# Two of four v chunk pairs by Strassen's seven products, bias by an adding DMA, in a two-layer decoder trunk

## The chip, the core and the metric

The kernel runs on one core of a Trainium2 chip. The metric is the device time of one execution in microseconds (us), the median of several runs. The engines named below are PE (TensorE: matmuls and transposes), PEld (its weight loads), DVE (VectorE), ACT (ScalarE), POOL (GpSimd) and SP (SyncE, which issues DMAs here). Each engine works through its own instructions in a fixed order and waits where an input is not there yet.

## What is computed

The input is one sequence of 256 rows of width 2048. Layer one is attention: RMS norm, an input projection, two mixers with a bias on the scores, an output projection and the residual. Layer two, in which most of the change lies, is this, cut from the reference:

```python
h = _rms(x, ln_g)                               # 256 x 2048
z = h @ w_in                                    # w_in: 2048 x 12288
uv = jax.nn.gelu(z[..., :2 * C_WIDTH])          # C_WIDTH = 4096
gate = jax.nn.silu(z[..., 2 * C_WIDTH:])
u, v = uv[..., :C_WIDTH], uv[..., C_WIDTH:]
v = _rms(v, v_g)                                # needs all of a row of v
ws = w_s * np.tril(np.ones((128, 128)))
s = jnp.einsum('gts,bnsgc->bntgc', ws, v) + b_s
y = u * s * gate
return x + y @ w_out                            # w_out: 4096 x 2048
```

## The kernel before

All products are made from float32 values split in two parts, a rounded high part (hi, type fp32r) and the rest (lo). A product is then three matmuls: hi x hi, hi x lo of the weights, lo x hi of the weights (L121 to L123).

`gemm` works on one **chunk**, 512 columns of a weight matrix. The rows stand in two halves of 128 (two accumulators in PSUM, one for each half), and the 2048 of the inner dimension in 16 k tiles of 128. `wtile` loads two k tiles of weights at a time (512 KB, on SP's queue, L81, six buffers `wraw`), ACT rounds them into `whi` (L85) and DVE subtracts to get `wlo` (L86), four buffers each. One such tile feeds 2 k tiles x 2 halves x 3 = 12 matmuls of 128x512, so a chunk has 96.

The first layer: input projection chunks, with attention spread between their matmuls by `fill()`, which takes one step of a queue of generators. Each of eight `bias_tile` calls loads 512 KB of bias on POOL's queue (L271) and adds the mask with POOL (L272). Then comes the output projection of four chunks (lines from L541). After each, `resid` adds the accumulators to the residual `xr` (DVE L518) and takes squares (ACT L520); `next_hT` transposes the new `xr` (PE L529, four transposes into one PSUM bank, two banks in a chunk), and makes from it, in pieces of 128x256, `hTh` (ACT L535, scaled) and `hTl` (DVE L536), the left side of the next layer. The last of the four chunks thus has its `next_hT` after it, among the matmuls of the first v chunk. `row_rstd` makes the row scale from a chain of tiny DVE operations.

The second layer begins with the eight v chunks (the **v stage**, from 436 us on): a gemm, Gelu by ACT (L191), squares (L574), load of v_g on POOL's queue (L576), multiplication by it on POOL (L577). All v tiles stay in SBUF. After the eighth, the row scale of v is known, and for each of eight chunks come u and gate gemms with the spatial mixing `sgu` between their matmuls; then the last projection, `w_out1`.

The instructions are put on the engines in an order that a scheduler makes ahead of time from the program; the rows of that order are shown in the section on the change.

Of the kernel before, what the change touches and what calls it, by code (L numbers as in the profile page):

```python
# [33 lines left out]
def trunk(ctx, tc, x, xT, ev_g, w_in0, w_kva, qk_g, sinks, w_out0, od_g, w_in1, v_g, w_sT, b_s,  # L34
# [8 lines left out]
    ps = ctx.enter_context(tc.tile_pool(name="ps", bufs=4, space=bass.MemoryType.PSUM))  # L43
# [13 lines left out]
    def psum(tag, bufs):  # L57
        return ps.tile([P, 512], F32, tag=tag, bufs=bufs, name=nm(tag))
# [16 lines left out]
    def wtile(w, kt, cw, fine=False):  # L75
# [7 lines left out]
        for j in range(0, 2, step):  # L83
            js = slice(j, j + step)
            nc.scalar.copy(hi[:, js, :cw], raw[:, js, :cw])  # L85
            nc.vector.tensor_tensor(lo[:, js, :cw], raw[:, js, :cw], hi[:, js, :cw].bitcast(F32),  # L86
                                    op=ALU.subtract)
        return hi, lo
# [11 lines left out]
    def gemm(aT, nkt, w, cw, pre=None, last=False):  # L100
# [25 lines left out]
        return acc if last else [g[0] for g in acc]  # L126

# [393 lines left out]

    def next_hT(q):
        hi, lo = c4([P, 4, S], nm("hTh"), F32R), c4([P, 4, S], nm("hTl"), F32R)
        for p0 in range(0, 4, 2):
            tp = psum("s", 2)
# [5 lines left out]
            for j in range(2):  # L531
                kt = 4 * q + p0 + j
                gk = g1[:, kt:kt + 1]
                src = tp[:, j * 256:(j + 1) * 256]
                nc.scalar.activation(hi[:, p0 + j, :], src, AF.Copy, scale=gk)  # L535
                nc.vector.scalar_tensor_tensor(lo[:, p0 + j, :], src, gk,  # L536
                                               hi[:, p0 + j, :].bitcast(F32),
                                               op0=ALU.mult, op1=ALU.subtract)
            if p0:
                hT1[q] = (hi, lo)  # L540
            yield  # L541

# [11 lines left out]
    nc.scalar.dma_start(bst, b_s)  # L554

# [10 lines left out]
    in1 = lambda c: gemm(yTk(hT1), KT, w_in1[c], 512)  # L566
    ssv = cons.tile([P, 2, 8], F32, name="ssv")
    vt = []
    for c in range(8):
        acc = in1(8 + c)  # L570
        v = evac(acc, 512, AF.Gelu, rs=rs1, name="v")
        for tt in range(2):
            junk = m2([P, 512], nm("junk"))
            nc.scalar.activation(junk, v[:, tt, :], AF.Square, accum_out=ssv[:, tt, c:c + 1])  # L574
        gv = m2([P, 512], nm("gv"))
# [121 lines left out]
```

## Time and profile before

| | us |
|---|---|
| median of 3 runs (1158.7 to 1159.94) | 1159.05 |
| the profiled execution | 1158.9 |
| its span, first to last instruction | 1157.1 |
| PE busy in it | 1149.3 |
| DVE busy | 641.3 |
| ACT busy | 592.7 |
| POOL busy | 115.5 |

The difference between the execution and its span lies around the program, before its first and after its last instruction. In a row of the timeline the first number is the start in us from the start of the span, the second the busy time, then engine, line, operation, tile written from tiles read, its shape, and in square brackets how long the engine had been idle before it and what ended that. The ends of matmuls are modelled: one row is 0.39 us long where the next starts 0.23 us later, so the distance of starts is what a matmul costs. A row with x2 or x4 is several instructions in one.

### The profile page before, as it was taken

The page shows a single profiled execution, that of the slowest core. Times are in us where ns is not written, and L with a number is a line of the kernel's source. Part 1 is how long each engine was busy: PE and PEld are TensorE (multiplying, and loading weights), DVE is VectorE, ACT ScalarE, POOL GpSimd, SP SyncE. Part 2 cuts the span into 40 slices and gives each one's busy share as a digit, 9 for nine tenths or more (in the row PEclk, how much of TensorE's full clock was granted, in tenths as well). Part 3 has the DMA queues.
Part 4 walks back from the last instruction along what each step waited for, and adds up shares of the span by engine and source line. Part 5 has one row for each costly group of instructions (what it writes and reads, how often), then busy time and mean ns, then how long its engine had stood idle before and what let it go on. Part 6 is the DMA issues. An engine that isn't in the chain of part 4 may idle for free.

```text
span 1157.1 us, 14468 instructions
## 1 busy us (share of the span) xinstructions
PE 1149.3 (99%) x5498; PEld 952.8 (82%) x5498; DVE 641.3 (55%) x823; ACT 592.7 (51%) x820; POOL 115.5 (10%) x69
## 2 busy tenths in 40 slices
PE   9999999999999999999999999999999999999998
PEld 7887787788788888888888888888888888888887
DVE  6586567556546565544546555555555555445443
ACT  6556664644654455445445445554554455333432
POOL 0132112113012000111110000000000000000000
PEclk9999999999999999999999999999999999999999
DMA  9676435546447555666666555555556555666661
GB/s 352 224 248 208 130 117 184 172 137 226 144 143 228 185 183 182 215 204 200 213 203 193 184 181 187 177 184 194 185 168 197 182 184 172 203 207 210 197 210 38
DMA packets 63638, 218.37 MB, mean 189 GB/s; under 512 B 7632, under 2 KB 10320, under 8 KB 63312
## 3 DMA queue, kind: packets, MB, share of 16 engines
q1 hardware_dynamic: 60352, 209.74, 56.2%
q0 software_dynamic: 2080, 7.34, 2.1%
q8 instruction: 43, 0.70, 0.2%
q10 hardware_dynamic: 1136, 0.36, 0.1%
q14 instruction: 27, 0.22, 0.1%
HBM read 215.32 MB, written 2.10 MB: 188 GB/s over the span
## 4 chain that ended last, share of the span: by engine, by line
PE 95%; DVE 1%; ACT 1%; DMA 1%; issue 1%; SPq 0%; ACTq 0%
PE g L121 30%; PE g L122 30%; PE g L123 30%; PE t L331 1%; DMA wraw<-in_w_in_dram 1%; ACT whi L85 1%; DVE wlo L86 1%; PE s L298 1%; PE u L347 1%; PE u L346 1%; PE t L385 1%; PE u L345 0%; PE t L218 0%; PE s L599 0%; PE s L600 0%
## 5 line engine op out<-in xcount | busy, mean ns | idle before, releaser
L86 DVE TENSOR_TENSOR wlo<-wraw,whi 128x1024 fp32r<-128x1024 f32 (+1 forms) x393 | 512.7, 1309 | 448.8 <-ACT whi L85 447.7
L85 ACT CAST whi<-wraw 128x1024 fp32r<-128x1024 f32 (+1 forms) x393 | 408.3, 1041 | 490.8 <-PE g L123 468.0
L121 PE MATMUL g<-whi,hTh 128*128 128x512 f32 (+1 forms) x1184 | 464.2, 392 | 0.0
L122 PE MATMUL g<-wlo,hTh 128*128 128x512 f32 (+1 forms) x1184 | 459.5, 388 | 0.6 <-DVE wlo L86 0.6
L123 PE MATMUL g<-whi,hTl 128*128 128x512 f32 (+1 forms) x1184 | 458.9, 388 | 0.0
L123 PEld LDWEIGHTS g<-whi,hTl 128*128 128x128 f32 x1184 | 222.6, 188 | 45.0
L121 PEld LDWEIGHTS g<-whi,hTh 128*128 128x128 f32 x1184 | 222.8, 188 | 44.6
L122 PEld LDWEIGHTS g<-wlo,hTh 128*128 128x128 f32 x1184 | 222.8, 188 | 44.0 <-DVE wlo L86 1.4
L121 PE MATMUL g<-whi,yTh 128*128 128x512 f32 (+1 forms) x416 | 156.2, 376 | 0.0
L122 PE MATMUL g<-wlo,yTh 128*128 128x512 f32 (+1 forms) x416 | 155.3, 373 | 0.0
L123 PE MATMUL g<-whi,yTl 128*128 128x512 f32 (+1 forms) x416 | 155.3, 373 | 0.0
L123 PEld LDWEIGHTS g<-whi,yTl 128*128 128x128 f32 x416 | 78.3, 188 | 14.1
L121 PEld LDWEIGHTS g<-whi,yTh 128*128 128x128 f32 x416 | 78.4, 188 | 13.6
L122 PEld LDWEIGHTS g<-wlo,yTh 128*128 128x128 f32 x416 | 78.4, 189 | 13.5
L608 POOL TENSOR_TENSOR y<-y,gt 128x1024 f32<-128x1024 f32 x8 | 19.2, 2404 | 344.9 <-ACT gt L191 344.9
L577 POOL TENSOR_TENSOR v<-v,gv 128x1024 f32<-128x1024 f32 x8 | 22.1, 2757 | 219.5 <-ACT junk L574 219.5
L191 ACT ACT_TABLE_LOAD x20 | 25.7, 1283 | 1.7 <-PE g L123 1.4
L272 POOL TENSOR_TENSOR bias<-bias,ba 128x1024 f32<-128x1024 f32 x8 | 21.9, 2738 | 31.1 <-DMA bias<-in_bias_dram 27.8
L321 ACT ACTIVATE pr<-sb,nmx 128x256 f32<-128x256 f32 x32 | 16.2, 506 | 9.9 <-DVE nmx L319 6.6
L333 ACT COPY pt<-t 128x384 f32<-128x384 f32 x32 | 15.0, 469 | 9.8 <-PE t L331 9.8
L307 DVE CUSTOM_DVE_ANT_0 sb<-s,bias 128x256 f32<-128x256 f32 x32 | 13.3, 414 | 9.1 <-PE s L301 8.1
L588 DVE SCALAR_TENSOR_TENSOR vl<-v,rstdv,vh 128x512 fp32r<-128x512 f32 x16 | 11.3, 749 | 12.4 <-ACT vh L587 12.4
(127 smaller groups left out, 555.2 us busy)
## 6 DMA issues: line engine op xcount, KB each, us to landing
wraw<-in_w_in_dram SPq DMA_DIRECT2D x287, 512.0 KB, 3.7
wraw<-in_w_out_dram SPq DMA_DIRECT2D x96, 512.0 KB, 4.0
bias<-in_bias_dram POOLq DMA_DIRECT2D x8, 512.0 KB, 3.8
xT<-in_xT_dram SPq DMA_DIRECT2D x8, 256.0 KB, 5.0
xr<-in_x_dram SPq DMA_DIRECT2D x2, 1024.0 KB, 11.1
wraw<-in_w_kva_dram SPq DMA_DIRECT2D x8, 256.0 KB, 3.4
gv<-in_v_g_dram POOLq DMA_DIRECT2D x8, 256.0 KB, 3.1
out_dram<-o SPq DMA_DIRECT2D x7, 256.0 KB, 5.1
```

Of the source, the lines that this page charges most:

```text
L85: nc.scalar.copy(hi[:, js, :cw], raw[:, js, :cw])
L86: nc.vector.tensor_tensor(lo[:, js, :cw], raw[:, js, :cw], hi[:, js, :cw].bitcast(F32), op=ALU.subtract)
L121: nc.tensor.matmul(o, ah[:, sl], whi[:, k, a:b], start=st, stop=False)
L122: nc.tensor.matmul(o, ah[:, sl], wlo[:, k, a:b], start=False, stop=False)
L123: nc.tensor.matmul(o, al[:, sl], whi[:, k, a:b], start=False, stop=en)
L191: nc.scalar.activation(z[:, tt, :cw], acc[tt][:, :cw], func, scale=rs[:, tt:tt + 1])
L272: nc.gpsimd.tensor_tensor(bt, bt, ba[:, mix:mix + 1, :].broadcast_to([P, 4, 256]), op=ALU.add)
L307: nc.vector.tensor_tensor_reduce(out=sb[:, 0:256], in0=sp[:, 0:256], in1=bt[:, j, :], scale=1.0, scalar=NEG, op0=ALU.add, op1=ALU.max, acc ...
L321: nc.scalar.activation(pr[:, 0:256], sb[:, 0:256], AF.Exp, bias=nmx[:, j, 1:2], accum_out=l[:, j, 1:2])
L333: nc.scalar.copy(pt, tp[:, 0:384])
L577: nc.gpsimd.tensor_tensor(v, v, gv.unsqueeze(1).broadcast_to([P, 2, 512]), op=ALU.mult)
L608: nc.gpsimd.tensor_tensor(y, y, gate[0], op=ALU.mult)
```

## The change

The eight v chunks are chunks 8 to 15 of `w_in1`. Chunks 8 and 9 form a pair, and so do 12 and 13; chunks 10, 11, 14 and 15 stay plain. With rows halved (a1*, a2*), the inner dimension halved by even and odd k tiles, and the two chunks as column halves, a pair is a 2 x 2 block product, and `four_chunks` computes it by seven products instead of eight:

- p1 = a11 b11, p2 = a12 b21, p3 = (sum 3) b22, p4 = a22 t4, p5, p6, p7 = three sums of the left side times t1, t2, t3;
- t1 = the two even blocks, t3 = the two odd blocks, of one chunk plus the other, each made by a plain load on SP and a second load on POOL's queue that adds to it (`accum_op=ALU.add`); t2 = t1 + b22 and later t4 = t2 + b21 by DVE; the sums of the left side by DVE in `sums`, four operations and a split for each quarter of the inner dimension;
- the inner dimension goes in four steps s of four k tiles. Each step of the first phase has five products (30 matmuls) and two weight tiles of a plain chunk x (24); each of the second phase has two products (12) and two tiles of a plain chunk y (24);
- at the end of the five products p1 is copied by ACT, and u2, xs, u3 and the two v sums are made by DVE; then Gelu, squares and the multiplication by v_g follow as for a plain chunk.

Each v tile is written to HBM by POOL's queue and read back as `vc` in `sgu`. `next_hT` now makes a plain float32 tile `hf` by ACT first, then splits it as a whole (128x1024) into `hTh` and `hTl`. The transposes go to one bank `m` instead of two `s`. PSUM banks are given by a table. In `bias_tile` ACT copies the mask into the tile and the load of the bias adds to it. The spatial weights `ws` are prepared after the v stage instead of before it.

```diff
+    banks = {"g": [0, 1, 2, 3], "s": [4, 5], "t": [6], "u": [7], "x": [5, 6], "m": [7],
+             "p1": [0], "p5": [1], "p7": [2], "p6": [3], "p3": [4], "p2": [0], "p4": [3]}
...
+    def split(raw):
+        hi = wpool.tile([P, 2, 512], F32R, tag="whi", name=nm("whi"))
+        lo = wpool.tile([P, 2, 512], F32R, tag="wlo", name=nm("wlo"))
+        nc.scalar.copy(hi, raw)
+        nc.vector.tensor_tensor(lo, raw, hi.bitcast(F32), op=ALU.subtract)
         return hi, lo
...
+    def pair_load(w, c0, c1, s):
...
+        b11, t1, b22, t3 = rawt(), c4([P, 2, 512], nm("t1")), rawt(), c4([P, 2, 512], nm("t3"))
+        for t, c, k in ((t1, c0, 0), (t3, c1, 0), (b11, c0, 0), (b22, c1, 1)):
+            nc.sync.dma_start(t, blk(c, k))
+        nc.gpsimd.dma_start(t1, blk(c1, 0), accum_op=ALU.add)
+        nc.gpsimd.dma_start(t3, blk(c1, 1), accum_op=ALU.add)
+        return b11, t1, b22, t3
...
+            t2 = c4([P, 2, 512], nm("t2"))
+            t2s.append(t2)
+            for p, raw in (("p1", b11), ("p5", t1), ("p3", b22), ("p6", t2), ("p7", t3)):
+                if s == 0:
+                    bank[p] = psum(p)
+                if p == "p6":
+                    nc.vector.tensor_tensor(t2, t1, b22, op=ALU.add)
+                product(bank[p], a[p], split(raw), s, s == 0, s == n - 1)
+            if s == n - 1:
+                p1, u2, xs, u3 = (m2([P, 512], nm(k)) for k in ("p1", "u2", "xs", "u3"))
+                nc.scalar.copy(p1, bank["p1"])
+                nc.vector.tensor_tensor(u2, p1, bank["p6"], op=ALU.subtract)
+                nc.vector.tensor_tensor(xs, u2, bank["p5"], op=ALU.add)
+                nc.vector.tensor_tensor(u3, u2, bank["p7"], op=ALU.add)
+                take_neg(c1, (xs, xs), (bank["p3"], bank["p7"]))
...
-        nc.gpsimd.dma_start(bt, bias[(mix * 16 + h) // 4].rearrange("p (h k) -> p h k", h=4))
-        nc.gpsimd.tensor_tensor(bt, bt, ba[:, mix:mix + 1, :].broadcast_to([P, 4, 256]), op=ALU.add)
+        nc.scalar.copy(bt, ba[:, mix:mix + 1, :].broadcast_to([P, 4, 256]))
+        nc.gpsimd.dma_start(bt, bias[(mix * 16 + h) // 4].rearrange("p (h k) -> p h k", h=4),
+                            accum_op=ALU.add)
...
+        hi, lo = c4([P, 4, S], nm("hTh"), F32R), c4([P, 4, S], nm("hTl"), F32R)
+        nc.scalar.copy(hi, hf)
+        nc.vector.tensor_tensor(lo, hf, hi.bitcast(F32), op=ALU.subtract)
+        hT1[q] = (hi, lo)
+        yield
+        sT1[q] = sums(hf)
...
+        nc.gpsimd.tensor_tensor(v, v, gv.unsqueeze(1).broadcast_to([P, 2, 512]), op=ALU.mult)
+        nc.gpsimd.dma_start(vt[c], v)
...
+    for c in (8, 12):
+        four_chunks(yTk(hT1), sTk(sT1), w_in1, c, c + 1, c + 2, c + 3, take, take_neg, take2,
+                    (w_in1, c + 4, c + 5) if c == 8 else None)
...
+        vc = c4([P, 2, 512], nm("vc"))
+        nc.gpsimd.dma_start(vc, vt[c])
```

PE has 5104 rows in the order after where it had 5152. Three places of the order follow, in rows of line, operation, tile written, tiles read and shape (the digits behind a name count the tiles; t2821 is tile t2 number 821). The first is DVE where the v stage begins; before, right after the last residual adds (L518) come a weight tile's `wlo`, the chain of the row scale and a 128x256 `hTl`:

```order
L518 TENSOR_TENSOR xr_96<-g766_3730,xr_96 128x512
L518 TENSOR_TENSOR xr_96<-g767_3731,xr_96 128x512
L86 TENSOR_TENSOR wlo824_4018<-wraw822_4015,whi823_4017 128x1024
L181 TENSOR_REDUCE rstd1s_3902<-ss1_3216 128x2
L63 TENSOR_SCALAR ra798_3904<-rstd1s_3902 128x2
L65 TENSOR_SCALAR ry799_3906<-ra798_3904 128x2
L536 SCALAR_TENSOR_TENSOR hTl813_3954<-s814_3955,g1_3214,hTh812_3953 128x256
```

and now, from the `wlo` of t1 on (the eleven rows of the row scale's chain are the part left out):

```order
L103 TENSOR_TENSOR wlo829_4003<-t1814_3962,whi828_4002 128x1024
L103 TENSOR_TENSOR wlo833_4021<-wraw815_3963,whi832_4020 128x1024
L651 TENSOR_TENSOR xr_98<-g774_3748,xr_98 128x512
L651 TENSOR_TENSOR xr_98<-g775_3749,xr_98 128x512
...
L713 TENSOR_SCALAR nrs1_3950<-rstd1_3944 128x2
L674 TENSOR_TENSOR hTl835_4031<-hf825_3993,hTh834_4030 128x1024
L224 TENSOR_TENSOR t2821_3981<-t1814_3962,wraw815_3963 128x1024
L684 TENSOR_TENSOR sf839_4046<-hf825_3993 128x256
...
L103 TENSOR_TENSOR wlo838_4037<-t2821_3981,whi837_4036 128x1024
L103 TENSOR_TENSOR wlo844_4057<-t3816_3964,whi843_4056 128x1024
L690 TENSOR_TENSOR sl841_4052<-sf839_4046,sh840_4051 128x1024
```

The residual adds moved behind the `wlo` of t1 and b22, and the t2 sum stands behind the whole `hTl`, ahead of the four sums.

The second is PE at the same place; before, four transposes stood among plain matmuls:

```order
L123 MATMUL g807_3939<-whi810_3943,hTl708_3401 128x512
L529 MATMUL s814_3955<-ident_91,xr_96 128x128 x4
L121 MATMUL g808_3940<-whi810_3943,hTh707_3400 128x512
L122 MATMUL g808_3940<-wlo811_3944,hTh707_3400 128x512
L123 MATMUL g808_3940<-whi810_3943,hTl708_3401 128x512
```

and now between the products p1, p5 and p3 of step 0, with p6 and p7 behind:

```order
L188 MATMUL p1822_3982<-whi823_3983,hTl714_3436 128x512
L665 MATMUL m826_3994<-ident_93,xr_98 128x128 x4
L186 MATMUL p5827_4001<-whi828_4002,sh716_3450 128x512
...
L665 MATMUL m830_4012<-ident_93,xr_98 128x128 x4
L188 MATMUL p3831_4019<-whi832_4020,sl717_3451 128x512
L186 MATMUL p3831_4019<-whi832_4020,sh716_3450 128x512
L187 MATMUL p3831_4019<-wlo833_4021,sh716_3450 128x512
L188 MATMUL p3831_4019<-whi832_4020,sl717_3451 128x512
L186 MATMUL p6836_4034<-whi837_4036,sh716_3450 128x512
L186 MATMUL p7842_4055<-whi843_4056,sh716_3450 128x512
L187 MATMUL p6836_4034<-wlo838_4037,sh716_3450 128x512
```

The second four transposes now have six p5 matmuls ahead of them, and p6 stands right behind p3.

The third is ACT at the end of the five products of the first pair; before, the end of a v chunk was

```order
L191 ACT_TABLE_LOAD
L191 ACTIVATE v837_4105<-g807_3939,rstd1_3918 128x512
L191 ACTIVATE v837_4105<-g808_3940,rstd1_3918 128x512
L574 ACTIVATE junk838_4108,ssv_3938<-v837_4105 128x512
L574 ACTIVATE junk839_4110,ssv_3938<-v837_4105 128x512
L85 CAST whi853_4173<-wraw852_4171 128x1024
```

and now it is

```order
L94 CAST whi935_4451<-wraw934_4449 128x1024
L736 ACT_TABLE_LOAD
L736 ACTIVATE v910_4360<-v910_4360,nrs1_3950 128x512 x2
L723 ACTIVATE junk911_4365,ssv_3952<-v910_4360 128x512
L723 ACTIVATE junk912_4367,ssv_3952<-v910_4360 128x512
L323 ACTIVATE v921_4411<-x845_4066,rstd1_3944 128x512
L323 ACTIVATE v921_4411<-x846_4067,rstd1_3944 128x512
L723 ACTIVATE junk922_4414,ssv_3952<-v921_4411 128x512
L723 ACTIVATE junk923_4416,ssv_3952<-v921_4411 128x512
L94 CAST whi938_4469<-wraw937_4467 128x1024
```

Two v tiles come to ACT in one piece there, the pair's (v910) and the plain chunk's (v921), between the first and the second `whi` of chunk y.

## Rows read from the trace of the kernel before

**Rows 1.** The page: the span, the engines, the granted clock in 40 slices (9 is full).

```profile
span 1157.1 us, 14468 instructions
...
PE 1149.3 (99%) x5498; PEld 952.8 (82%) x5498; DVE 641.3 (55%) x823; ACT 592.7 (51%) x820; POOL 115.5 (10%) x69
...
PEclk9999999999999999999999999999999999999999
```

**Rows 2.** The page: the chain that ended last, its share by engine.

```profile
PE 95%; DVE 1%; ACT 1%; DMA 1%; issue 1%; SPq 0%; ACTq 0%
```

**Rows 3.** The timeline of PE, at the start of the v stage.

```profile
437.23 0.60 PE L529 MATMUL s<-ident,xr 128*128 128x128 f32 x4
...
441.12 0.39 PE L122 MATMUL g<-wlo,hTh 128*128 128x512 f32 x1
441.35 0.40 PE L123 MATMUL g<-whi,hTl 128*128 128x512 f32 x1
```

**Rows 4.** The timeline of DVE and of POOL in the v stage.

```profile
506.12 2.42 DVE L86 TENSOR_TENSOR wlo<-wraw,whi 128x1024 fp32r<-128x1024 f32 x1 [0.92 <-ACT whi L85]
...
511.56 1.22 DVE L86 TENSOR_TENSOR wlo<-wraw,whi 128x1024 fp32r<-128x1024 f32 x1 [1.50 <-ACT whi L85]
514.27 1.23 DVE L86 TENSOR_TENSOR wlo<-wraw,whi 128x1024 fp32r<-128x1024 f32 x1 [1.50 <-ACT whi L85]
...
504.65 2.81 POOL L577 TENSOR_TENSOR v<-v,gv 128x1024 f32<-128x1024 f32 x1 [18.43 <-ACT junk L574]
```

**Rows 5.** Windows: us, then each engine's busy time (instructions), granted clock, DMA share, GB/s.

```profile
7.00:14.00 7.00, 6.43 (x26) 4.64 (x26) 4.69 (x8) 4.64 (x8) 0.00 (x0) 1.00 1.04 386
90.00:145.00 55.00, 53.43 (x309) 42.70 (x307) 31.62 (x77) 37.18 (x77) 8.62 (x6) 1.00 0.48 157
481.00:503.00 22.00, 22.00 (x98) 18.21 (x97) 10.99 (x8) 11.20 (x16) 3.33 (x2) 1.00 0.67 205
```

**Rows 6.** The waits of PE: who waited for whom, us in total, times, longest us.

```profile
PE t L218 <- ACT q L234: 1.2, 1, 1.2
...
PE g L122 <- DVE wlo L86: 0.6, 2, 0.4
```

**Rows 7.** The timeline of ACT at ends of v chunks.

```profile
457.14 1.28 ACT L191 ACT_TABLE_LOAD   x1
...
500.95 0.69 ACT L191 ACTIVATE v<-g,rstd 128x512 f32<-128x512 f32 x1 [0.31 <-PE g L123]
501.67 0.63 ACT L574 ACTIVATE junk<-v 128x512 f32<-128x512 f32 x1
...
510.47 1.05 ACT L85 CAST whi<-wraw 128x1024 fp32r<-128x1024 f32 x1 [1.66 <-PE g L123]
```

**Rows 8.** The timeline of DVE, then of ACT, behind the last out-projection chunk.

```profile
435.57 1.28 DVE L518 TENSOR_TENSOR xr<-g,xr 128x512 f32<-128x512 f32 x2
...
438.86 0.48 DVE L536 SCALAR_TENSOR_TENSOR hTl<-s,g,hTh 128x256 fp32r<-128x256 f32 x1
...
438.25 0.46 ACT L535 ACTIVATE hTh<-s,g 128x256 fp32r<-128x256 f32 x1
...
440.26 0.83 ACT L535 ACTIVATE hTh<-s,g 128x256 fp32r<-128x256 f32 x2
```

**Rows 9.** The page: DMA issues, KB each, median us from issue to landing.

```profile
wraw<-in_w_in_dram SPq DMA_DIRECT2D x287, 512.0 KB, 3.7
...
bias<-in_bias_dram POOLq DMA_DIRECT2D x8, 512.0 KB, 3.8
```

**Rows 10.** POOL's groups by line (mean ns), and the timeline of DVE in attention.

```profile
L272 POOL TENSOR_TENSOR bias<-bias,ba 128x1024 f32<-128x1024 f32 x8 | 21.9, 2738 | 31.1 <-DMA bias<-in_bias_dram 27.8 <-PE g L123 3.3
...
97.76 2.53 DVE L86 TENSOR_TENSOR wlo<-wraw,whi 128x1024 fp32r<-128x1024 f32 x1 [1.49 <-ACT whi L85]
```

**Rows 11.** The timeline of PE, the kernel's first 128x512 matmuls.

```profile
5.77 1.20 PE L121 MATMUL g<-whi,hTh 128*128 128x512 f32 x2
6.77 0.53 PE L122 MATMUL g<-wlo,hTh 128*128 128x512 f32 x1
```

More of the change, by code (lines that the diff above doesn't have):

```diff
@@ new lines, in pair_load2, with product @@
+    def pair_load2(w, c0, s):
+        b21 = wpool.tile([P, 2, 512], F32, tag="wraw", bufs=6, name=nm("wraw"))
+        nc.sync.dma_start(b21, w[c0][2 * s:2 * s + 2, :, 512:1024].rearrange("j p n -> p j n"))
+        return b21
+    def product(bank, a, parts, s, start, stop):
+        hi, lo = parts
+        for r in range(2):
+            ah, al = a(2 * s + r)
+            nc.tensor.matmul(bank, ah, hi[:, r, :], start=start and r == 0, stop=False)
+            nc.tensor.matmul(bank, ah, lo[:, r, :], start=False, stop=False)
+            nc.tensor.matmul(bank, al, hi[:, r, :], start=False, stop=stop and r == 1)
+        fill()
@@ new lines, in chunk_step @@
+    def chunk_step(acc, aT, w, k0, nkt):
+        whi, wlo = wtile(w, k0, 512)
+        for tt in range(2):
+            for k in range(2):
+                ah, al = aT(k0 + k)
+                sl = slice(tt * P, (tt + 1) * P)
+                st, en = k0 + k == 0, k0 + k == nkt - 1
+                nc.tensor.matmul(acc[tt], ah[:, sl], whi[:, k, :], start=st, stop=False)
+                nc.tensor.matmul(acc[tt], ah[:, sl], wlo[:, k, :], start=False, stop=False)
+                nc.tensor.matmul(acc[tt], al[:, sl], whi[:, k, :], start=False, stop=en)
+            fill()
@@ L520, in resid @@
             nc.scalar.activation(junk, xs, AF.Square, accum_out=ss1[:, tt, q:q + 1])
+    sT1 = [None] * 4
     def next_hT(q):
[L523 removed]
+        hf = c4([P, 4, S], nm("hf"))
         for p0 in range(0, 4, 2):
[L525 removed]
+            tp = psum("m")
             for j in range(2):
@@ L532, in next_hT, with sums, sTk, get @@
                 kt = 4 * q + p0 + j
[L533 to L540, printed above, removed]
-            yield
+                nc.scalar.activation(hf[:, p0 + j, :], tp[:, j * 256:(j + 1) * 256], AF.Copy,
+                                     scale=g1[:, kt:kt + 1])
+            yield
+        hi, lo = c4([P, 4, S], nm("hTh"), F32R), c4([P, 4, S], nm("hTl"), F32R)
[4 more added lines that the diff above has]
+        sT1[q] = sums(hf)
+    def sums(hf):
+        e = hf.rearrange("p (j k) (t n) -> p j k t n", k=2, t=2)
+        a11, a12, a21, a22 = (e[:, :, k, t, :] for t in range(2) for k in range(2))
+        sf = c4([P, 4, 2, P], nm("sf"))
+        tt = nc.vector.tensor_tensor
+        tt(sf[:, 0], a22, a21, op=ALU.subtract)
+        tt(sf[:, 1], sf[:, 0], a11, op=ALU.add)
+        tt(sf[:, 2], a11, a21, op=ALU.subtract)
+        tt(sf[:, 3], sf[:, 1], a12, op=ALU.subtract)
+        sh, sl = c4([P, 4, 2, P], nm("sh"), F32R), c4([P, 4, 2, P], nm("sl"), F32R)
+        nc.scalar.copy(sh, sf)
+        nc.vector.tensor_tensor(sl, sf, sh.bitcast(F32), op=ALU.subtract)
+        return sh, sl
+    def sTk(sT):
+        def get(q):
+            while sT[q] is None:
+                fill()
+            return sT[q]
+        return get
     for q in range(4):
@@ L564, in trunk @@
         ws.append((wsh, wsl))
[L566 to L575, printed above, removed]
-        nc.gpsimd.dma_start(gv, v_g[:, c * 512:(c + 1) * 512])
-        nc.gpsimd.tensor_tensor(v, v, gv.unsqueeze(1).broadcast_to([P, 2, 512]), op=ALU.mult)
-        vt.append(v)
     rsv = row_rstd(ssv, CW, "rstdv")
```

87 lines of the change are left out of this document (82 added, 5 removed).

## The prediction, made before the changed kernel was run

> **What bounds the kernel now.** I read the page first. The span is 1157.1 us and TensorE is busy for 1149.3 of it, at the full granted clock in every slice [rows 1]. The chain of work that ended last lies on PE for 95% [rows 2]. So the time is a count of matmuls, plus the few places where PE waits. Next I read the spacing of the 128x512 matmuls in the timeline: starts at 441.12 and 441.35, and twelve of them (one weight tile) between two weight splits on DVE at 511.56 and 514.27, so 2.71/12 = 0.226 us each [rows 3, 4]. Then the windows: in the v stage (481 to 503) PE is busy for 22.00 of 22.00 us, DVE for 10.99 and ACT for 11.20, and the DMA engines for 0.67 of the time at 205 GB/s [rows 5]. PE waits for nobody there. In the list of waits over the whole span the longest of PE is 1.2 us, a q transpose of the first layer, and its waits for wlo come to 0.6 us together [rows 6]. The profiled execution took 1158.9 us (span and 1.8 us around it), the median of three runs is 1159.05. The sum below is made against 1158.9; what it gives for the median differs by 0.15 us.
>
> **Matmuls removed: -10.9 us.** One pair of chunks needed 2 chunks x 16 k tiles x 2 row halves x 3 split terms = 192 matmuls. Seven products of eight k steps and three terms need 168. Two pairs do this: 48 matmuls fewer, all 128x512, 48 x 0.226 = 10.9 us. That is on the path as long as PE stays full.
>
> **What DVE and ACT get in exchange.** In the steady part of a pair one step is 5 products x 6 + 24 matmuls of the plain chunk = 54 matmuls, 12.2 us. It wants seven whi casts of 1.05 us on ACT (7.4 us) and seven wlo plus one t2 sum of 1.22 us on DVE (9.8 us) [rows 4, 7]. Both fit, with four buffers of whi and wlo ahead of PE, so I cost this at nothing. If POOL's multiply by v_g runs beside a DVE subtraction, that subtraction takes 2.42 instead of 1.22 us [rows 4]; the step still fits (11.0 of 12.2).
>
> **The start of the v stage: +9.0 us (7.4 to 12).** This is the largest unknown. Before, the last quarter of the residual is turned into hTh and hTl in pieces of 128x256 (0.46 us ACT, 0.48 DVE), while PE has twelve k tiles of finished input to work on, and nothing waits [rows 8]. After, the product p6 wants t2 = t1 + b22, and the order puts the t2 sum on DVE behind the residual adds, the rstd chain and the last hTl. From the end of the last out-projection matmul (zero), laying the rows of the order end to end with these durations: the second residual add ends at 1.0; PE's first four transposes stand behind two p3 and six p1 matmuls and end at 2.25, the second four behind six p5 matmuls, at 4.1 (0.226 a matmul, about 0.45 for four transposes [rows 3]); the two pairs of hf copies end at 5.2 (0.83 for two); the one-piece hTh cast of 1.05 ends near 6.2 and hTl (1.22) at 7.4; the t2 sum at 8.65; its whi at 9.75. PE has 18 matmuls and eight transposes, so it runs dry at 5.0 and waits 4.8 us. Then four sums (4 x 0.48) stand ahead of wlo of t2, which ends at 11.75; wlo of t3 at 13.0, sl at 14.25, and the two plain tiles' wlo at 15.5 and 16.7. The step ends at 20.5 where 54 matmuls and the transposes would have ended at 13.1: 7.4 us. On top comes the adding DMA: t1 is loaded once, and its second load is issued only after the first has landed. A 512 KB load lands in 3.7 us, one on POOL's queue in 3.8 [rows 9], and t1's wlo stands in front of the residual adds on DVE. SP issues the first load behind one that waits for a weight buffer of the last out-projection chunk, so it lands about 7.5 us before zero, and the second 3 to 1.6 us before zero. Behind it come one whi (1.05), two wlo (2.45) and the two adds (1.28): the adds end 0.85 to 2.2 us later than the 1.0 above. I take 1.6. The upper end, 12, has the adding load landing 3 to 4 us later still, as if it took twice its 3.8. A cover that could shrink all this is that DVE takes the rows in another order; the order excludes that.
>
> The Trainium skill, "DMA: Bandwidth & Descriptors", section "Rules for kernel authors", says that an accumulating DMA reads its destination and writes it later, so that one depending on an earlier load must wait for that load's semaphore. It speaks against this change where the first load is late; no trace of the kernel before has such a DMA, and the sum above takes its price from the two loads' rows alone.
>
> **The three epilogues: +5.5 us (3.4 to 7).** At the end of the five products DVE makes u2, xs, u3 and two v sums of about 0.64 us each [rows 8], and ACT loads a table (1.28) and runs four Gelus (0.69) and four squares (0.63), 6.6 us in one piece before the second whi of chunk y [rows 7]. PE has p2, p4 and one y tile in hand, 24 matmuls, 5.4 us. Laying the order's rows end to end gives 1.3 us without and 2.4 with POOL's multiply beside DVE. I take 2.4, since the multiply of 2.81 us [rows 4] comes right then. The passage from pair one to pair two has the same burst ahead of the whi of p3, behind which t2's sum stands: 1.7 (1.1 to 2). The epilogue of pair two: 1.4 (1.0 to 2.6). Before, the corresponding burst of two Gelus and two squares is hidden, PE shows no idle in 481 to 503 [rows 5].
>
> **Transfers.** A pair reads 28 blocks of 512 KB instead of 16, and v goes out and back (4.2 MB each way). In a steady step 8 blocks move in 12.2 us, 344 GB/s; the start of the kernel sustained 386 GB/s [rows 5]. So the loads fit, just. If an adding load costs twice its bytes the step needs 10 blocks, 13.6 us, 1.4 over, on the two or three steps of each pair that aren't prefetched: 5 us. I take 0.3. The v blocks are written long before they are read; vc has a chunk of 96 matmuls (21.7 us) between its load and its use, and a load of that size lands in about 4.
>
> **Attention bias: 0 (-2 to +2).** POOL loses 8 adds of 2.74 us, one of which stretched a wlo to 2.53 us; ACT gets 8 copies of about 1.05 [rows 10]. The longest wait of PE there is 1.2 us [rows 6]; some may go, others may come from ACT, whose share in that stage is 37.2 of 55.0 us [rows 5]. ws preparation moved behind the v stage, extra casts and sums in the out-projection: each has several tiles of PE work above it, 0 (to 0.5).
>
> **Sum.** -10.9 + 9.0 + 5.5 + 0.3 = +3.9 on 1158.9, so 1162.8, in round numbers 1163.
>
> **Rivals.** (a) *The matmuls show* (faster). The start and the epilogues cost less than 10.9 - 2.3 = 8.6 together: for example the four whi buffers carry the epilogues (0 to 1 each) and the t1 load is early, so the start is 7.4 alone. 1158.9 - 10.9 + 7.4 + 0.5 = 1156, down to 1152 if attention gains 2 and the start is shortened to 5. Against it: the start's chain is a string of dependent rows, none of which can overlap another. (b) *The bill is even*: start 7.4 and epilogues at their lower end, 3.4: 1158.8. (c) *Adding loads bound the stage* (slower still). From twice the bytes on: 5 us, and 3.8 at the start: 1172. For it: 344 of 386 GB/s are wanted already. Against: half of each block's steps (two products) need only 3 blocks in 8.1 us. (d) *The clock falls.* Before, it never leaves the full level [rows 1], and only the first two 128x512 matmuls of the kernel take a whole microsecond together, 0.50 each against 0.226 later [rows 3, 11]. If the 4.8 us in which PE is dry leave it at the lower of its two levels (1.2 and 2.4 GHz), each of the 36 matmuls behind costs up to 0.226 more, but DVE paces these anyway (15.5 us for 8.2 us of matmuls): 1 to 3 us, 1165. The Trainium skill, "TensorE: Matmul & The Clock Gate", section "HAM oscillation — how this bites in real kernels", says that an idle stretch lets the clock fall and that the next burst begins cold; the trace of before has no such gap in its middle to agree or differ. That the change doesn't remove the matmuls can be ruled out: the order has 48 fewer.
>
> **How the numbers follow.** Forecast with its own spread 1160.5 to 1167: 0.45. (a) 0.15, (b) 0.18, (c) 0.10, (d) 0.12. About 0.2%, 2.3 us, is what a measurement of this kernel can tell from no change. Faster by more than that, below 1156.7: 0.15. Within, up to 1161.4: (b) and the foot of the forecast, 0.22. Slower: 0.63. The range for 8 in 10: 1156 to 1171.
>
> **What would show it.** In the timeline after: PE idle for 4 to 6 us before the first p6 product, waiting for whi of t2, with DVE's t2 sum behind hTl. If PE waits instead for t1 or t3 by DMA, the adding load is the cause. At each epilogue PE waits 1 to 3 us for wlo or whi. In the steady step PE should be full and DVE busy for 10 of 12.2 us; a PE there that waits for DMA speaks for (c). The granted clock right behind the gap decides (d). In attention the wait rows should change by less than 2 us. The forecast is wrong if the gap at the start is under 3 us, or if the adding loads land in more than 8 us.

## The result and the profile after

The changed kernel takes 1194.49 us (median of 4, 1193.14 to 1195.48) where the kernel before takes 1159.48: a ratio of 1.0302, with a 95% interval of 1.0284 to 1.032. The direction was forecast, the size was not: +35 us instead of +4, far outside the range. The page of the profiled execution (1195.48 us):

```profile
span 1193.7 us, 14566 instructions
...
PE 1155.9 (97%) x5450; PEld 949.8 (80%) x5450; DVE 695.1 (58%) x886; ACT 631.3 (53%) x862; POOL 123.6 (10%) x93
...
PEclk9999999999999988899899999999999999999999
...
PE 85%; DMA 6%; DVE 4%; ACT 3%; issue 2%; POOL 0%; SPq 0%; POOLq 0%; ACTq 0%; DVEq 0%
```

Beside [rows 1, 2]: there are 48 matmuls fewer, as the order said, yet PE's busy time is longer, the granted clock is below 9 in four slices of the v stage, and the chain now holds 6% DMA where it held 1%. The waits of PE (who waited for whom: us in total, times, longest) show where; [rows 6] had nothing over 1.2:

```profile
PE p L187 <- DVE wlo L103: 16.8, 8, 8.9
PE p L186 <- ACT whi L102: 10.4, 5, 5.2
PE x L199 <- DVE wlo L95: 2.4, 1, 2.4
```

I count a loss as follows: the distance from each matmul's start to the next, less the usual distance of its kind (0.227 us for 128x512), summed over the v stage (434 to 640). Before it is 1.5 us there, after 45.9; outside the v stage the two agree within 2 us. With the 10.9 us of matmuls that are gone, 45.9 - 1.5 - 10.9 = 33.5 of the 36.6 us between the spans; the usual distance is known to 1 ns only and thousands of matmuls carry it, so such a sum is good to some 3 us. Of the 45.9, 31.7 are waits of more than 0.7 us and 13.4 lie in 62 small steps of 0.1 to 0.7 us. Most of these small steps (51, together 11.0 us) are matmuls at the lower level of the clock behind a wait. By place (an **adding load** is one of the 16 loads with `accum_op=ALU.add` that make t1 and t3):

| place | loss, us | what PE waited for |
|---|---|---|
| 434 to 449 | 8.3 | t1's adding load, first step of pair one |
| 449 to 462 | 7.9 | the t2 sum behind hTl |
| 462 to 495 | 8.2 | adding loads of steps two and three |
| 512 to 530 | 5.3 | the epilogue of the five products |
| 550 to 592 | 15.3 | adding loads of pair two |

The start, on PE, then ACT and DVE (timeline):

```profile
435.95 0.39 PE L139 MATMUL g<-whi,yTl 128*128 128x512 f32 x1
441.55 0.80 PE L186 MATMUL p<-whi,sh 128*128 128x512 f32 x1 [5.21 <-ACT whi L102]
...
449.24 0.39 PE L188 MATMUL p<-whi,sl 128*128 128x512 f32 x1
454.17 0.79 PE L186 MATMUL p<-whi,sh 128*128 128x512 f32 x1 [4.55 <-ACT whi L102]
...
456.29 0.63 PE L188 MATMUL p<-whi,sl 128*128 128x512 f32 x1
456.72 0.63 PE L186 MATMUL p<-whi,sh 128*128 128x512 f32 x1
...
439.50 1.04 ACT L102 CAST whi<-t 128x1024 fp32r<-128x1024 f32 x1 [10.24 <-DMA t<-in_w_in_dram]
...
450.68 1.23 DVE L674 TENSOR_TENSOR hTl<-hf,hTh 128x1024 fp32r<-128x1024 f32 x1 [3.00 <-ACT hTh L673]
451.82 1.22 DVE L224 TENSOR_TENSOR t<-t,wraw 128x1024 f32<-128x1024 f32 x1
```

The first wait ends when whi of t1 can be cast: ACT had been idle for 10.24 us until t1's adding load landed at 439.5, 3.5 us after the last out-projection matmul. The second, 449.24 to 454.17, is the one that the prediction worked out (4.8 us): it measures 4.93 less a matmul's 0.23, 4.7. Behind it matmuls start 0.43 us apart (456.29, 456.72) instead of 0.227. In pair two the t2 sum stands at the head of DVE's queue until the adding load of t1 has landed, and the `wlo` rows behind it wait with it:

```profile
575.22 1.23 DVE L224 TENSOR_TENSOR t<-t,wraw 128x1024 f32<-128x1024 f32 x1 [8.21 <-DMA t<-in_w_in_dram]
```

The page's DMA issues (KB each, us to landing), against [rows 9]:

```profile
wraw<-in_w_in_dram SPq DMA_DIRECT2D x279, 512.0 KB, 3.8
...
t<-in_w_in_dram SPq DMA_DIRECT2D x16, 512.0 KB, 7.2
t<-in_w_in_dram POOLq DMA_DIRECT2D x16, 512.0 KB, 12.2
bias<-in_bias_dram POOLq DMA_DIRECT2D x8, 512.0 KB, 5.9
```

An adding load of a weight block takes 12.2 us to land. Three stretches of the DMA view say what it costs the engines (queue: packets, MB, share of the 16 engines' time). First 442.5 to 445.5, where adding loads run alone, then 455 to 458, plain loads of the same 2 KB pieces alone, then 571 to 576, both:

```profile
DMA packets 321, 0.62 MB, mean 207 GB/s; under 512 B 18, under 2 KB 18, under 8 KB 321
...
q0 software_dynamic: 321, 0.62, 113.2%
...
DMA packets 615, 1.19 MB, mean 398 GB/s; under 512 B 32, under 2 KB 32, under 8 KB 615
...
q1 hardware_dynamic: 615, 1.19, 104.9%
...
DMA packets 673, 1.31 MB, mean 262 GB/s; under 512 B 34, under 2 KB 34, under 8 KB 673
...
q0 software_dynamic: 337, 0.66, 70.8%
q1 hardware_dynamic: 336, 0.65, 39.2%
```

Adding moves half as much in the same time (207 against 398 GB/s). In engine time (share x 16 engines x length / packets) that is 0.17 us for an adding packet and 0.08 for a plain one. In the third stretch both queues get the same number of packets, 337 and 336, so there a plain load beside an adding one moves no faster than that one: 262 GB/s for both together.

### The profile page after: what moved, and what is told of

Read it like the earlier page. It is cut to its first block, busy times and chain, and to the rows that moved or that the text cites. A ratio compares the mean times of both kernels' runs of the same rounds, so it can differ in the third digit from the quotient of the medians.

```text
span 1193.7 us, 14566 instructions
## 1 busy us (share of the span) xinstructions
PE 1155.9 (97%) x5450; PEld 949.8 (80%) x5450; DVE 695.1 (58%) x886; ACT 631.3 (53%) x862; POOL 123.6 (10%) x93
## 4 chain that ended last, share of the span: by engine, by line
PE 85%; DMA 6%; DVE 4%; ACT 3%; issue 2%; POOL 0%; SPq 0%; POOLq 0%; ACTq 0%; DVEq 0%
PE g L137 24%; PE g L138 23%; PE g L139 23%; DMA t<-in_w_in_dram 4%; PE p L187 2%; PE p L188 1%; PE x L199 1%; PE x L200 1%; PE p L186 1%; PE x L198 1%; DVE wlo L95 1%; ACT whi L94 1%; DVE wlo L103 1%; PE t L464 1%; DMA wraw<-in_w_in_dram 1%
## 5 line engine op out<-in xcount | busy, mean ns | idle before, releaser
L95 DVE TENSOR_TENSOR wlo<-wraw,whi 128x1024 fp32r<-128x1024 f32 (+1 forms) x361 | 463.5, 1288 | 382.1 <-ACT whi L94 381.6
L137 PE MATMUL g<-whi,hTh 128*128 128x512 f32 (+1 forms) x928 | 363.8, 392 | 0.2 <-ACT whi L94 0.2
L138 PE MATMUL g<-wlo,hTh 128*128 128x512 f32 (+1 forms) x928 | 360.0, 388 | 0.7 <-DVE wlo L95 0.5
L139 PE MATMUL g<-whi,hTl 128*128 128x512 f32 (+1 forms) x928 | 359.3, 387 | 0.0
L137 PEld LDWEIGHTS g<-whi,hTh 128*128 128x128 f32 x928 | 174.4, 188 | 35.4 <-ACT whi L94 0.7
L138 PEld LDWEIGHTS g<-wlo,hTh 128*128 128x128 f32 x928 | 174.6, 188 | 34.5 <-DVE wlo L95 1.7
L139 PEld LDWEIGHTS g<-whi,hTl 128*128 128x128 f32 x928 | 174.4, 188 | 34.7
L102 ACT CAST whi<-t 128x1024 fp32r<-128x1024 f32 x32 | 33.5, 1051 | 39.3 <-DMA t<-in_w_in_dram 18.8
L199 PE MATMUL x<-wlo,hTh 128*128 128x512 f32 x128 | 50.5, 394 | 2.4 <-DVE wlo L95 2.4
L200 PE MATMUL x<-whi,hTl 128*128 128x512 f32 x128 | 50.3, 393 | 0.0
L198 PE MATMUL x<-whi,hTh 128*128 128x512 f32 x128 | 50.0, 393 | 0.2 <-ACT v L323 0.2
L187 PE MATMUL p<-wlo,sh 128*128 128x512 f32 x64 | 29.4, 459 | 16.5 <-DVE wlo L103 16.5
## 6 DMA issues: line engine op xcount, KB each, us to landing
t<-in_w_in_dram POOLq DMA_DIRECT2D x16, 512.0 KB, 12.2
```

The source lines that it names most:

```text
L102: nc.scalar.copy(hi, raw)
L137: nc.tensor.matmul(o, ah[:, sl], whi[:, k, a:b], start=st, stop=False)
L138: nc.tensor.matmul(o, ah[:, sl], wlo[:, k, a:b], start=False, stop=False)
L139: nc.tensor.matmul(o, al[:, sl], whi[:, k, a:b], start=False, stop=en)
L187: nc.tensor.matmul(bank, ah, lo[:, r, :], start=False, stop=False)
L198: nc.tensor.matmul(acc[tt], ah[:, sl], whi[:, k, :], start=st, stop=False)
```

## Experiments: the adding loads

Theory A: the second loads of t1 and t3 are the loss. **Left out** (t1 and t3 keep one block):

```diff
-        nc.gpsimd.dma_start(t1, blk(c1, 0), accum_op=ALU.add)
-        nc.gpsimd.dma_start(t3, blk(c1, 1), accum_op=ALU.add)
```

> The changed kernel without the second, adding loads of t1 and t3: the sums t1 and t3 keep one block each, so part of the product is left out. All else is as in the changed kernel. In its trace PE stood for 31.8 us more than its matmuls need at the places where t1, t3 or a sum of them was awaited (8.3 at 434 to 449, 8.2 at 462 to 495, 15.3 at 550 to 592), 7.9 at the t2 sum behind hTl and 5.3 at the first epilogue. Theory A (the adding loads are what is late): those 31.8 go, 1194.5 - 31.8 = 1163 us, and the 4.7 us gap behind hTl stays. Rival B (the first loads are late already, behind SP's queue and the bytes of the pairs): the waits stay to more than half, 1180 us or more.

1163.54 us, as theory A had it, and by chance what was forecast for the whole change. The loss in the v stage falls from 45.9 to 16.5: 8.3 at the start, 4.9 at the first epilogue, 3.3 behind it. Its waits in the v stage:

```profile
PE p L184 <- ACT whi L102: 4.8, 2, 4.5
PE x L197 <- DVE wlo L95: 2.1, 1, 2.1
PE p L185 <- DVE wlo L103: 1.7, 3, 0.8
```

**The second loads overwrite instead of adding:**

```diff
-        nc.gpsimd.dma_start(t1, blk(c1, 0), accum_op=ALU.add)
-        nc.gpsimd.dma_start(t3, blk(c1, 1), accum_op=ALU.add)
+        nc.gpsimd.dma_start(t1, blk(c1, 0))
+        nc.gpsimd.dma_start(t3, blk(c1, 1))
```

> The second loads stay on POOL's queue, in the same place, with the same bytes, and still wait for the first, but they overwrite instead of adding (so t1 and t3 hold one block, part of the product is left out). Theory A1 (the add itself is dear: its 2 KB packets take 0.176 us in the trace where plain ones take 0.083 to 0.098): the loads land in 5 to 6 us instead of 12.2 and half or more of the 31.8 us goes, 1165 to 1178 us. Rival A2 (two loads in series and the issue on POOL are the cost, whatever they do with the data): 1188 to 1195 us.

1183.29 us, between the two theories. The second loads land in 7.8 us instead of 12.2. The add itself is 1194.5 - 1183.3 = 11.2 us, the rest of the second loads still 20.

**The same bytes, waiting for nothing and for nobody:**

```diff
-        nc.gpsimd.dma_start(t1, blk(c1, 0), accum_op=ALU.add)
-        nc.gpsimd.dma_start(t3, blk(c1, 1), accum_op=ALU.add)
+        for k in range(2):
+            sc = c4([P, 2, 512], nm("sc"))
+            nc.gpsimd.dma_start(sc, blk(c1, k))
```

> As the run without the second loads (1163.5 us), but the same two blocks are read, plainly, into tiles that nobody uses, on POOL's queue, waiting for no first load. The bytes of the changed kernel without the add and without the two loads in series. With plain overwriting second loads it was 1183.3. Theory S (the wait in series makes the loads late): 1163 to 1168. Theory V (the volume of data fills the DMA engines and delays all loads): 1176 to 1184.

1175.13 us: 11.6 above the run without them, just under theory V's range and far above theory S's. Most of it is one wait in pair two, where the DMA engines were full (1.01 of their time at 374 GB/s from 533 to 552). PE waited for the `wlo` of a plain tile, and on DVE that row stood behind a t2 sum whose plain b22 load was late:

```profile
PE x L200 <- DVE wlo L95: 12.6, 2, 10.1
...
560.53 1.23 DVE L225 TENSOR_TENSOR t<-t,wraw 128x1024 f32<-128x1024 f32 x1 [11.24 <-DMA wraw<-in_w_in_dram]
```

This run also answers whether POOL's queue is slow as such. From 544 to 547 its plain loads ran alone and moved 369 GB/s, against 207 with the add:

```profile
DMA packets 302, 1.11 MB, mean 369 GB/s; under 512 B 35, under 2 KB 35, under 8 KB 301
...
q0 software_dynamic: 301, 1.09, 95.9%
```

So the 31.0 us of the second loads (1163.5 to 1194.5) are three shares: 11.6 for their volume, 8.2 for standing in series behind the first load with somebody waiting for them, 11.2 for the add. By the ratios to the kernel before, measured beside each run, they are 10.9, 8.7 and 10.7, so each is good to about 1 us. They are differences between runs whose waits lie in different places, so they don't say which row of the table by place belongs to which share. Two things were not told apart: the scratch tiles take buffers of the large pool, so the first share may hold a part that is buffers; and plain packets on POOL's queue are larger than adding ones (1.09 MB in 301 packets, against 0.62 in 321), so the last share holds that as well.

**The first pair's loads a chunk earlier** (adding loads kept):

```diff
+        if q == 3:
+            pre_pair[(id(w_in1), 8)] = pair_load(w_in1, 8, 9, 0)
         acc = gemm(yTk(yT0), KT, w_out0[q], 512)
```

> The changed kernel with the first pair's first loads written ahead of the last out-projection chunk instead of behind it. Theory: the 8.3 us at 434 to 449, where t1's add lands 3.5 us after the last out-projection matmul, go for the most part: 1186 to 1189 us, and the 4.7 us gap behind hTl stays. Rival (the late add there only covers other waits, which then show): 1192 to 1195.

1185.26 us, 9.2 less: the first wait is gone, the 4.7 us gap behind hTl stands, and so do the later ones. Lateness at the start was a matter of when the load was issued.

**Sums by DVE, no adding load:**

```diff
-        for t, c, k in ((t1, c0, 0), (t3, c1, 0), (b11, c0, 0), (b22, c1, 1)):
+        for t, c, k in ((t3, c1, 0), (b11, c0, 0), (b22, c1, 1)):
             nc.sync.dma_start(t, blk(c, k))
-        nc.gpsimd.dma_start(t1, blk(c1, 0), accum_op=ALU.add)
-        nc.gpsimd.dma_start(t3, blk(c1, 1), accum_op=ALU.add)
...
+            nc.vector.tensor_tensor(t1, b11, t3, op=ALU.add)
...
+                if p == "p7":
+                    nc.vector.tensor_tensor(t3, t3, b22, op=ALU.add)
```

> t1 and t3 are summed by DVE from the blocks b11, b12 and b22 that are loaded once each; no adding load, and one block of four less to read. DVE then needs 7 splits and 3 sums of 1.22 us, 12.2 us for a step in which PE needs 12.2. Theory A: the 31.8 us go and DVE gives some back, 2.4 us at the start and 0 to 1.5 in each of eight steps: 1166 to 1176 us. Rival B (loads late anyway): 1180 or more. Rival C (DVE becomes the bound and its lateness adds up with the epilogues): 1180 or more too, but with PE waiting for DVE alone and no DMA in the waits.

1168.67 us, in theory A's range: 26 us better than the change, 10 worse than the kernel before (ratio 1.0084). A step of the first phase reads five blocks here instead of eight. (By the code, t3 is the sum of the two blocks of the second chunk, not of the two odd blocks, as the section on the change has it; so b12 is loaded once and serves t1 and t3.)

**The bias alone, on the kernel before,** and **the change without any pair** (`take(c, in1(c))` for all eight chunks):

> The kernel before with the change to the attention bias alone (ACT copies the mask, the load of the bias adds to it). By all theories of the v stage this is apart from them: within 2 us of before, 1157.5 to 1161.5. Should it be 5 us slower or more, part of the loss of the whole change lies in the attention and not in the v stage.

> The changed kernel with all eight v chunks plain: what is left of the change is the bias, v kept in HBM, hf split in one piece with the four sums of each quarter (made, and not used), and ws behind the v stage. Theory (all of that is hidden, the loss is in the pairs): 1158 to 1161 us. Rival (these parts cost something of their own, which was put down to the pairs): 1163 or more.

Ratios to the kernel before of 0.9995 (0.9984 to 1.0005) and 1.0001 (0.9992 to 1.001). The bias, v in HBM, hf and the later ws cost and gain nothing by themselves, to 0.1%, though the bias loads land in 5.6 us there instead of 3.8. All of the loss comes with the pairs.

## Experiments: what is left without adding loads

**The last quarter's chain behind the first step's products**, so that the t2 sum no longer stands behind hTl:

```diff
-        fill()
+        if not (start and late):
+            fill()
...
+                product(bank[p], a[p], split(raw), s, s == 0, s == n - 1, late=c0 == 8)
```

> The kernel with t1 and t3 summed by DVE (1168.7 us), and in the first step of the first pair the products take no step of the waiting generators, so that the transposes, hf, hTh and hTl of the last quarter come behind p7 and the t2 sum no longer stands behind hTl on DVE. Theory: that place cost 4.7 us of gap and about 3 us of matmuls at the lower clock behind it; both go, 1160 to 1162 us, and the granted clock stays at the upper level there. Rival (DVE has 12.2 us of work in a step of 12.2, so hTl and the sums of the last quarter only move the wait to a later step): 1166 us or more, with a new wait of PE for wlo between 445 and 490.

1168.93 us, no gain over the run with sums on DVE: the rival was right that the wait moves, but not for its reason. DVE was not full there; it stood idle in the same chain, which PE now met 10 us later (timeline of DVE):

```profile
448.86 1.23 DVE L676 TENSOR_TENSOR hTl<-hf,hTh 128x1024 fp32r<-128x1024 f32 x1 [3.49 <-ACT hTh L675]
...
452.66 1.23 DVE L692 TENSOR_TENSOR sl<-sf,sh 128x1024 fp32r<-128x1024 f32 x1 [1.11 <-ACT sh L691]
```

**t4 in one rotating buffer, the plain chunk's Gelu first:**

```diff
-                take_neg(c1, (xs, xs), (bank["p3"], bank["p7"]))
...
         take(x, accx)
+        take_neg(c1, (xs, xs), (bank["p3"], bank["p7"]))
...
+            t4 = wpool.tile([P, 2, 512], F32, tag="t4", bufs=1, name=nm("t4"))
+            nc.vector.tensor_tensor(t4, t2, cur, op=ALU.add)
```

> As the one before, and in addition: t4 is written into one rotating buffer, so that only one sum for t4 can run ahead, the Gelu of the plain chunk comes before that of the pair, and one 4 KB buffer fewer is in the large pool. Theory (the first epilogue's gap of 2.8 us comes from DVE, where t4 sums that wait for b21's load stand ahead of the wlo that PE wants, and 2 us of lower clock come with it): 4 to 5 us less than the one before, 1155 to 1158, faster than the kernel before. Rival (ACT's burst of Gelus and squares is what is late): within 1.5 us of the one before.

1165.87 us, 3 better than the run before, where 4 to 5 were expected; the forecast of 1155 to 1158 went far too low, because it built on the expected gain of that run. What remained at the epilogue was a DVE operation beside POOL's multiply (timelines of DVE and POOL):

```profile
500.47 3.44 DVE L95 TENSOR_TENSOR wlo<-wraw,whi 128x1024 fp32r<-128x1024 f32 x1 [3.63 <-ACT whi L94]
...
500.43 2.38 POOL L729 TENSOR_TENSOR v<-v,gv 128x1024 f32<-128x1024 f32 x1
```

**The multiply by v_g moved to the read-back tile** in the u and gate stage:

> As the run with t4 in one buffer and the other order (1165.9 us), but POOL's multiplication by v_g is taken from the v stage and done on the v tile that is read back in the u and gate stage. In that run's trace three DVE operations beside such a multiply took 3.3 to 3.4 us instead of 1.2, each right ahead of a wait of PE (2.3 us at 501, 1.0 and 1.8 at 532 to 540, 1.0 at 592). Theory (the two engines contend there): 3 to 5 us less, 1161 to 1163. Rival (the bursts on ACT are what is late, DVE's long operations only fill the wait): within 1.5 us of 1165.9.

1165.48 us: a miss. The waits at 501 (2.3) and 538 (1.8) did go, but new ones of 2.4 and 1.2 us came at 631, at the passage to the u chunks, and the loss in the v stage stayed at 18.4 (17.8 before this edit).

**The chain of the last quarter spread,** two steps of other work between its links:

```diff
         nc.scalar.copy(hi, hf)
+        for _ in range(w):
+            yield
         nc.vector.tensor_tensor(lo, hf, hi.bitcast(F32), op=ALU.subtract)
```

> As the one before it, and the chain of the last quarter (hTh on ACT, hTl on DVE, four sums, sh on ACT, sl on DVE) is written with two steps of other work between each of its links, so that DVE has rows ahead of hTl and sl that wait for nothing. Theory (DVE stood idle for 3.5 and 1.1 us in order behind that chain, and PE waited 5.3 us for it, wherever the chain was put): 6 to 7 us less than the one before, 1154 to 1157, faster than the kernel before. Rival (DVE has 12.2 us of work for each 12.2 us step, so the wait only moves on): 1160 or more.

1161.51 us, 4 better, where 6 to 7 were expected: four waits of about 1 us or less take the place of one of 5.3. Its twelve executions spread from 1156.74 to 1164.57, and the mean granted clock sorts them: 1156.7 to 1157.7 where it was 1.000 (three), 1159.7 and 1159.9 where it was 0.999, 1161.3 to 1164.6 where it was 0.996 or 0.997 (seven). The next run shows the same place at the other level.

**ws written behind the first u chunk:**

> As the run with the spread chain (1161.5 us median; its profiled execution, 1157.7, kept the upper clock throughout), with the preparation of the spatial weights ws written behind the matmuls of the first u chunk instead of ahead of them. In that run ACT's wsh stood ahead of the whi of the first u tiles and waited 4.6 and 6.5 us for POOL, and PE waited 2.3 us at 626. Theory: that wait goes, and no lower clock behind it: 2 to 3 us less, 1158 to 1160. Rival (another burst is right behind it): within 1 us of 1161.5.

1162.89 us, a miss: in the trace ACT still meets the ws rows ahead of the `whi` of the u tiles, and the wait at 628 stayed (ACT):

```profile
628.25 1.04 ACT L762 CAST wsh<-ws 128x1024 fp32r<-128x1024 f32 x1 [7.15 <-POOL ws L760]
```

But up to 457 us this run and the one before have the same waits (1.5 and 0.9 us between 449 and 457), and behind them the windows (us, busy time of each engine, granted clock, DMA) are, of the run before and then of this one:

```profile
457.00:464.00 7.00, 6.57 (x29) 5.46 (x30) 7.00 (x7) 4.17 (x5) 0.00 (x0) 1.00 0.54 184
...
457.00:464.00 7.00, 6.67 (x22) 5.37 (x23) 7.00 (x7) 3.33 (x4) 0.00 (x0) 0.76 0.54 195
```

The code up to there is the same in both runs; their 7 us hold 29 matmuls at 1.00 and 22 at 0.76.

**Adding loads in the first step of each pair alone, issued far ahead:**

> As the one before it, and in the first step of each pair, and there alone, t1 and t3 are summed by adding loads again, issued a whole out-projection chunk or two steps (16 us) ahead, where the DMA engines have room; DVE sums them in the other six steps. Theory (an adding load costs nothing where it is issued over 12 us ahead and the DMA engines aren't full, and DVE saves 2.44 us in each first step, where its lateness makes PE wait 3.5 us): 3 to 5 us less than the one before, 1154 to 1156, the upper clock in all runs, faster than the kernel before. Rival (the adding loads are late here too, or take the place of the plain ones): as the one before or slower, 1159 or more.

1164.87 us, a miss. The loads were not late for the first pair, but DVE's saved 2.44 us were not where it was late (it still has hTl and the four sums in one piece with the next step's rows, 448 to 457). At 512 a plain tile came late, and the DMA engines were full ahead of it: from 500 to 504 POOL's queue, with the second pair's two adding loads and a v block, took 97% of their time and SP's queue 6%:

```profile
513.06 1.04 ACT L94 CAST whi<-wraw 128x1024 fp32r<-128x1024 f32 x1 [7.64 <-DMA wraw<-in_w_in_dram]
```

**The second half of ws before the third u chunk:**

```diff
+        if c == 2:
+            ws_prep(1)
```

> Both pairs as in the run with the spread chain (1161.5 us), and the second half of ws, whose cast on ACT stood ahead of whi and waited 6.5 us for POOL, is prepared before the third u chunk. Theory: the wait of PE at 626 (2.3 us, and the lower clock behind it) goes: 1158 to 1160. Rival: the wait comes from the first half of ws or from v's row scale and stays, 1161 or more.

1157.13 us, ratio 0.9978 (0.9968 to 0.9987): the wait at 626 is gone, and both pairs together now beat the kernel before, by 2.3 us of the 10.9. That is 4.4 us less than the run with the spread chain, where 2 to 3 were expected; the mean granted clock was 0.998 or more in all ten executions, which may be the rest. Of the loss that is left in the v stage, about 6 us lie between 449 and 462, where the first pair meets the end of the out-projection.

**One pair alone,** the second, the rest as in that run:

```diff
-    for c in (8, 12):
-        four_chunks(yTk(hT1), sTk(sT1), w_in1, c, c + 1, c + 2, c + 3, take, take_neg, take2,
-                    (w_in1, c + 4, c + 5) if c == 8 else None)
+    for c in range(8, 12):
+        if c == 11:
+            pre_pair[(id(w_in1), 12)] = pair_load(w_in1, 12, 13, 0)
+        take(c, in1(c))
+    four_chunks(yTk(hT1), sTk(sT1), w_in1, 12, 13, 14, 15, take, take_neg, take2, None)
```

> One pair alone, chunks 12 and 13, sums by DVE, multiplication by v_g in the u and gate stage, chain of the last quarter spread, the second half of ws prepared before the third u chunk; chunks 8 to 11 plain. 24 matmuls fewer, 5.4 us. Theory (what is left of the loss lies where the first pair meets the end of the out-projection, where DVE has the residual, the row scale and the last quarter on top of 12.2 us of work in each 12.2 us step): the wait there goes, 1 to 2 us of wait stay at the pair's ends, 1154.5 to 1157, faster than before, at the upper clock in all runs. Rival (a pair costs what it saves wherever it stands): 1158.5 to 1161.

1155.81 us, ratio 0.9969 (0.9956 to 0.9981), five executions within 1.1 us, clock 0.999 or 1.000: the lowest median of all, with half of the matmuls saved. The run before lies 1.3 us above it, and the two intervals overlap. Its waits in the v stage are these alone:

```profile
PE p L184 <- ACT v L326: 0.3, 1, 0.3
PE g L138 <- DVE wlo L95: 0.3, 1, 0.3
PE p L185 <- DVE wlo L103: 0.2, 1, 0.2
PE p L184 <- ACT whi L102: 0.2, 1, 0.2
```

Against the run without pairs (loss 0.9 in the v stage) it loses 3.3 and saves 24 x 0.227 = 5.4: 1159.6 - 5.4 + 2.4 = 1156.6, measured 1155.8. So the second pair pays for itself, and the first pair costs about its gain, most of it where it meets the out-projection. The first pair alone, or two pairs that both stand away from that place, was not run.

## Why the prediction was wrong

**Matmuls, -10.9: right.** The trace has 48 fewer, and the run with one pair returns half of the 10.9 us less its waits.

**Bias and the rest, 0: right,** to 0.1% in two runs.

**The start: the chain was right, the load was not.** The gap behind hTl measures 4.7 for 4.8, and without the second loads the start loses 8.3 where the chain alone was put at 7.4. The term that failed is the lateness of t1: I had its second load land 3 to 1.6 us ahead of the last out-projection matmul, from the 3.8 us of a plain load on POOL's queue [rows 9]; it landed 3.5 us behind it. The "upper end" did name a landing 3 to 4 us later, which was still short: the start lost 8.3 + 7.9 us, the upper end was 12. Four adding loads were issued between 429.6 and 435.8 and shared the queue. The prediction's own sign of being wrong, adding loads that land in more than 8 us, is what came: 12.2.

**The epilogues, +5.5: the waits were about right, the small steps beside them were left out.** Without second loads the loss there is 4.9 at the first epilogue and 3.3 behind it, 8.2 in all. Of these, 3.3 are small steps, about half of them matmuls at the lower clock, and the rest waits, 4.9 where 5.5 were forecast. That POOL's multiply stretches a DVE row there was named rightly.

**Transfers, +0.3: this step failed, and it is the error.** I priced an adding load like a plain one, in the engines' time and in its landing; the second loads cost 31.0 us. Rival (c) had the mechanism, with a chance of 0.10 and 8.8 us, and its bound of twice the bytes is what the DMA view shows (207 against 398 GB/s). Its own sum was short as well: 1.4 us on two or three steps of each pair is 5.6 to 8.4 for two pairs, not 5.

Two things were missing. First, I compared the step's volume with 386 GB/s, a rate that plain loads reach by themselves [rows 5]. An estimate from the packet times above: a step's two adding blocks (512 packets at 0.17 us) and six plain ones (1536 at 0.08 to 0.09, the latter beside an adding load) take 16 engines 13.3 to 14.3 us instead of 12.2. Over the six steps of both pairs that are not prefetched that is 7 to 13 us, and the run that overwrites puts the add at 11.2. The places of these steps lost 23.5 us (8.2 and 15.3), so the engines' time alone does not explain them. Second, I summed the loads' time and left out that they stand in a row: the second load waits for the first on POOL's queue, the t2 sum for the second at the head of DVE's, the `wlo` of every other product behind it. The runs put the shares of volume, row and add at 11.6, 8.2 and 11.2 us.

The sentence of the Trainium skill that the prediction set aside, on the accumulating DMA that reads its destination and writes it later ("DMA: Bandwidth & Descriptors", section "Rules for kernel authors"), fits the view, in which an adding packet takes twice the engines' time of a plain one of the same size.

**The clock: right in kind, too small.** Rival (d) stood beside the forecast as a case of its own, at 1 to 3 us; but the clock fell behind every long wait, whatever caused it. Behind the waits of 3.6 to 8.9 us the granted clock of the stretch was 0.64 to 0.79, and in the whole v stage matmuls at the lower level cost 11.0 us (windows of the changed kernel):

```profile
454.00:462.00 8.00, 7.67 (x21) 5.62 (x22) 7.97 (x9) 6.02 (x7) 2.41 (x2) 0.64 0.73 236
...
577.50:590.00 12.50, 12.36 (x44) 10.03 (x45) 8.86 (x9) 4.58 (x5) 0.00 (x0) 0.79 0.92 255
```

I had priced it at the start alone, and taken DVE's pace there as cover. The Trainium skill, "TensorE: Matmul & The Clock Gate", section "HAM oscillation — how this bites in real kernels", has the burst behind an idle stretch begin cold; these rows agree.

What stays open: how much of the 11.6 us of volume is buffers, how much of the 11.2 us of the add is its smaller packets, and what decides whether the clock falls behind waits of about 1 us or less.

## What to carry to other kernels

Where a transfer replaces an addition, price it by what it does to the other transfers of that stretch and by who stands behind it in each queue, not by its own bytes: here 16 adding loads cost 31 us where summing on DVE cost 5 (1168.7 against 1163.5 us). On a full TensorE a long wait can be paid twice, once as a wait and once as matmuls at the lower clock behind it: here 31.7 us of waits brought 11.0 us of those. Work saved in a stage is worth most where its helpers have room: one pair in the middle of the stage gained at least as much as two with the first at a junction.

## What the runs showed of the hardware that I had not expected

- An adding DMA takes an engine twice as long for each 2 KB packet (207 against 398 GB/s alone). Its issue on POOL takes 1.20 us, where the same load without the add took 0.72.
- From 571 to 576 POOL's queue and SP's queue got the same number of packets (337 and 336), so slow packets on one slowed the other: 262 GB/s together.
- The same code with the same waits of 0.9 us or less ran on at the full clock in one traced execution and at 0.76 in another (29 against 22 matmuls in 7 us). Executions of one program at a mean clock of 0.996 or 0.997 took 3.7 to 7.8 us longer than those at 1.000.
- One `wlo` of 1.22 us took 3.44 us beside POOL's multiply, more than the doubling of [rows 4].
